# Tree attention: SyncE's store of heads 76 to 79 is cut by partitions for two heads instead of four

## The chip, the cores and the metric

The kernel runs on one core of a Trainium2 chip. A core has TensorE (PE) for matrix products, VectorE (DVE), ScalarE (ACT), GpSimd (POOL) and SyncE (SP), which only issues transfers and waits, and 16 DMA engines that move data between the chip's main memory and the core's on-chip memory. That on-chip memory has 128 partitions. SyncE, ScalarE and GpSimd each have a queue of transfers; all queues run on the same 16 DMA engines. In the profile q0 is GpSimd's queue (software_dynamic), q1 SyncE's and q10 ScalarE's (hardware_dynamic).

The metric is the device time of one execution in microseconds (us); lower is better. The kernel before takes 135.0 us, the median of three runs between 134.7 and 135.12 us.

## The reference

There are 8 x 12 = 96 heads, each with 512 positions of dimension 64. The mask is a binary tree: position i attends to itself and to its ancestors.

```python
for i in range(seq):
    mask[i, i] = 1
    parent = i
    while parent > 0:
        parent = (parent - 1) // 2
        mask[i, parent] = 1
scores = einsum('bhqd,bhkd->bhqk', Q, K) * scale + (1 - mask) * (-1e9)
weights = softmax(scores)
return einsum('bhqk,bhkd->bhqd', weights, V).astype(float32)
```

Inputs and output are float32, 96 x 512 x 64 each, 12.58 MB.

## The kernel before, in words

A position is written 4p + t: partition p holds positions 4p to 4p + 3 of a head. So one head's output takes 128 rows of 4 x 64 floats, one row of 1024 bytes for each partition, and a row is contiguous in main memory.

The heads are worked in 48 pairs. The main loop runs over i from 0 to 48. A step S computes the scores of pair i on TensorE (mask codes enter as a matrix product, `scores1` and `scores2`) and their exponentials on ScalarE; a step V multiplies the weights of pair i - 1 with its values (`values`, L661) and normalises (`norm`: reciprocal L691, multiplication L693, both on VectorE), which leaves float32 results in a tile `of`; steps K and Q turn keys and queries for later pairs. From pair 16 on, pair i holds heads 8(i // 4) + i % 4 and the one four above it, so that four pairs make eight consecutive heads, and these share one `of` tile.

The order is written out by hand; the program's text is the order on each engine. GpSimd loads all but the first inputs by a list of operations (`pool_program`), and issues the stores of finished groups of eight heads on its queue. Each operation on that list is issued once `ready` allows it.

The stores of the end are divided. GpSimd stores heads 72 to 75 (512 KB) and, last, heads 80 to 87 (1024 KB). SyncE stores the rest of the group in between, heads 76 to 79 (`APART` = 76), after step i = 41 (`APART_AT`), by `store_apart` (L711 to L714): one transfer for partitions 0 to 59 (`APART_ROWS` = 60) of all four heads, and one for the 68 partitions from 60 on. At steps 45, 46 and 47 SyncE stores two heads each (88 and 92, 89 and 93, 90 and 94), and after the loop head 91, while ScalarE stores head 95. SyncE's queue holds nothing else in this stretch; its transfers run in the order in which they are issued. At the end of the program SyncE waits for the stores (L918). All stores are issued by the helper `store`, so all have line L701.

The `of` tiles come from a pool of 11 buffers for 12 groups of heads, so the last group takes the buffer that the first group's store has left.

Of the kernel before, what the change touches and what calls it, by code (L numbers as in the profile page):

```python
# [119 lines left out]
def kernel(  # L120
# [7 lines left out]
    nc = tc.nc  # L128
# [571 lines left out]
    def store(eng, h0, n, step=1, p0=0, p1=P):  # L700
        return eng.dma_start(  # L701
            out=Or[p0:p1, h0:h0 + step * (n - 1) + 1:step, :],
            in_=ofs[h0 // 8][p0:p1, h0 % 8:h0 % 8 + step * (n - 1) + 1:step, :, :].rearrange(
                "p h t d -> p h (t d)"
            ),
        )


    APART, APART_AT, APART_ROWS = 76, 41, 60

    def store_apart():  # L711

        for p0, p1 in ((0, APART_ROWS), (APART_ROWS, P)):
            store(nc.sync, APART, 4, 1, p0, p1)  # L714

    def pool_program():

# [138 lines left out]
    for i in range(NP + 1):  # L856
# [29 lines left out]
        if i == APART_AT:  # L886
            store_apart()
# [35 lines left out]
```

## Time and profile before

| What | Value |
|---|---|
| Median of three runs | 135.0 us (134.7 to 135.12) |
| The profiled execution's own time | 134.66 us |
| Its span, first to last instruction | 132.9 us |
| TensorE busy | 114.7 us, 86% of the span |
| VectorE, ScalarE, GpSimd busy | 104.8, 101.1, 82.9 us |
| Read from and written to main memory | 37.94 MB and 12.58 MB, 380 GB/s over the span |
| SyncE's two transfers for heads 76 to 79 | issued from 111.66 us on, 240 KB and 272 KB |

Times inside the profile count from the span's start. A row of the timeline gives start, duration, engine, line and operation; a q behind an engine's name means its sequencer, which issues transfers. A row of DMA issues gives what goes where, the issuing engine, how many, the size of each, and the median time from issue to landing; it gives no landing where the records do not tell one. A row of a queue gives its packets, the megabytes, and the packets' time as a share of all 16 DMA engines' time in that stretch. A row of windows gives the stretch, the busy time of each engine with its instruction count, the clock granted to TensorE, and after it the mean busy share of the 16 DMA engines and what they moved in GB/s. Packet times in the records overlap by a few ns, so a share can stand slightly above the truth.

### The profile page before, as it was taken

What the parts mean: (1) busy time and instruction counts of PE and PEld (TensorE: products, weight loads), DVE (VectorE), ACT (ScalarE), POOL (GpSimd) and SP (SyncE); (2) the same over time, 40 slices, a digit from 0 to 9 for tenths busy, and PEclk for the clock granted to TensorE, in tenths of its full rate; (3) what the DMA queues carried; (4) which work ended last, traced back from release to release, by engine and by line L of the source; (5) the groups of instructions that cost most, each with busy time, mean ns of one, the idle gap of its engine ahead of it and who ended that gap; (6) DMA issues with size and microseconds to landing.
All of it is one profiled execution on the core that took longest, in us unless ns stands there. A gap on an engine that the chain in (4) does not pass through costs nothing.

```text
span 132.9 us, 5421 instructions
## 1 busy us (share of the span) xinstructions
PE 114.7 (86%) x2350; PEld 79.9 (60%) x2353; DVE 104.8 (79%) x254; ACT 101.1 (76%) x163; POOL 82.9 (62%) x114
## 2 busy tenths in 40 slices
PE   6983999999899798899999898994999999999900
PEld 2441677667576476667676675773676677775600
DVE  3436769988999998989899889896999977974530
ACT  4356469989799986969997797985799778789800
POOL 6968734345493999994399999926998935002000
PEclk9999599999999999999999999999999999999995
DMA  3999999999999999999999999999999999999980
GB/s 96 238 177 195 195 199 199 202 201 207 202 202 211 204 210 203 208 208 202 209 206 200 328 249 203 310 263 263 311 231 341 219 334 404 399 400 361 381 306 32
DMA packets 28092, 32.25 MB, mean 243 GB/s; under 512 B 1149, under 2 KB 23293, under 8 KB 28069
## 3 DMA queue, kind: packets, MB, share of 16 engines
q0 software_dynamic: 25696, 29.63, 109.9%
q1 hardware_dynamic: 1813, 1.83, 4.0%
q10 hardware_dynamic: 560, 0.46, 1.2%
q8 instruction: 18, 0.29, 0.8%
q14 instruction: 5, 0.04, 0.1%
HBM read 37.94 MB, written 12.58 MB: 380 GB/s over the span
## 4 chain that ended last, share of the span: by engine, by line
DMA 28%; PE 27%; DVE 19%; POOL 13%; issue 5%; ACT 4%; ACTq 0%; POOLq 0%
DMA qst<-in_Q_dram 19%; PE ob L661 9%; DMA vst<-in_V_dram 8%; POOL vt L370 7%; DVE of L693 6%; DVE vt L370 5%; PE s L566 4%; PE s L573 2%; DVE rec L691 2%; DVE kq L485 2%; PE ktp L469 2%; POOL kst L243 2%; PE s L611 2%; PE s L600 2%; DVE kq L489 1%
## 5 line engine op out<-in xcount | busy, mean ns | idle before, releaser
L583 ACT ACTIVATE e<-s 128x1024 bf16<-128x1024 f32 x40 | 40.9, 1023 | 14.0 <-PE s L573 13.6
L661 PE MATMUL ob<-vt,e 128*128 128x65 bf16 (+1 forms) x940 | 37.5, 198 | 2.7 <-DVE of L693 2.0
L661 PEld LDWEIGHTS <-e 128*128 128x128 bf16 (+1 forms) x960 | 30.5, 103 | 11.4 <-PE s L611 1.9
L370 POOL COPY vt<-vst 32x512 int32<-32x512 int32 (+4 forms) x44 | 32.4, 736 | 4.1 <-PE ob L661 1.9
L617 ACT ACTIVATE e<-s 128x384 bf16<-128x384 f32 x80 | 34.7, 491 | 0.0
L693 DVE TENSOR_TENSOR of<-ob,rec 128x512 f32<-128x512 f32 x47 | 32.5, 691 | 1.6
L370 DVE COPY vt<-vst 32x1024 bf16<-32x1024 bf16 (+5 forms) x47 | 22.8, 486 | 2.7 <-DMA vst<-in_V_dram 1.8
L691 DVE RECIPROCAL rec<-ob 128x8 f32<-128x8 f32 x47 | 9.6, 203 | 10.8 <-PE ob L661 9.7
L701 POOL DMA_DIRECT2D out_dram<-of x11 | 9.8, 892 | 9.2 <-DVE of L693 8.8
L573 PE MATMUL s<-qq,kq 64*128 64x512 bf16 x80 | 15.3, 377 | 0.0
L611 PEld LDWEIGHTS <-kq 64*128 64x128 bf16 x320 | 12.3, 94 | 4.1
L611 PE MATMUL s<-qq,kq 64*128 64x160 bf16 (+1 forms) x320 | 14.7, 208 | 0.0
L253 POOL DMA_DIRECT2D qst<-in_Q_dram x12 | 8.5, 705 | 6.8 <-DMA kst<-in_K_dram 3.2
L566 PE MATMUL s<-far,codes 40*128 40x512 bf16 x64 | 12.5, 386 | 0.1
L600 PEld LDWEIGHTS <-codes 40*128 40x128 bf16 x80 | 6.3, 95 | 9.7 <-issue 3.8
L542 DVE COPY qq<-qtp 128x1024 bf16<-128x1024 bf16 x16 | 10.9, 681 | 1.6 <-PE qtp L537 1.6
L370 ACT COPY vt<-vst 32x512 int32<-32x512 int32 (+3 forms) x19 | 10.4, 546 | 2.1 <-DMA vst<-in_V_dram 1.7
L579 ACT ACTIVATE e<-s 128x1024 bf16<-128x1024 f32 x8 | 8.2, 1022 | 5.0 <-PE s L573 4.8
L600 PE MATMUL s<-far,codes 40*128 40x384 bf16 x64 | 10.6, 324 | 0.5 <-ACT e L617 0.3
L476 PE MATMUL ktp<-ptile,kst 128*64 128x128 bf16 x256 | 10.1, 220 | 0.9 <-DMA kst<-in_K_dram 0.5
L253 POOL DMA_DIRECT2D kst<-in_K_dram x11 | 8.4, 768 | 3.9 <-DMA vst<-in_V_dram 1.9
L537 PE MATMUL qtp<-ptile,qst 128*64 128x128 bf16 x192 | 7.6, 220 | 2.5 <-DMA qst<-in_Q_dram 1.8
(56 smaller groups left out, 154.4 us busy)
## 6 DMA issues: line engine op xcount, KB each, us to landing
out_dram<-of POOLq DMA_DIRECT2D x10, 1024.0 KB, 15.7
kst<-in_K_dram POOLq DMA_DIRECT2D x9, 512.0 KB, 14.5
qst<-in_Q_dram POOLq DMA_DIRECT2D x8, 512.0 KB, 16.6
vst<-in_V_dram POOLq DMA_DIRECT2D x12, 256.0 KB, 12.9
vst<-in_V_dram POOLq DMA_DIRECT2D x6, 512.0 KB, 12.5
qst<-in_Q_dram POOLq DMA_DIRECT2D x6, 256.0 KB, 12.0
kst<-in_K_dram POOLq DMA_DIRECT2D x4, 256.0 KB, 9.7
out_dram<-of SPq DMA_DIRECT2D x3, 256.0 KB, 6.0
```

The lines of the kernel that those rows point to most:

```text
L253: return nc.gpsimd.dma_start(out=kept[b][:, h0 % KB:h0 % KB + n, :, :].rearrange("p (g x) t d -> p g (x t d)", x=x), in_=src[:, h0 // x:(h ...
L370: return copy(out=dst, in_=src)
L542: nc.vector.tensor_copy(out=qqs[j][:, :, 8 * last:8 * last + 8, :].rearrange("p b u c -> p b (u c)"), in_=quarters,)
L566: nc.tensor.matmul(out=sp[:, a, :], lhsT=(k1code if i < WIDE else k1wide)[64 * a:64 * a + CODE_ROWS, :], rhs=(q1code, q1wide, q1far)[(i >= ...
L573: nc.tensor.matmul(out=sp[:, a, :], lhsT=keys(i, a, TOP), rhs=qTs[i][64 * a:64 * a + 64, :, :].rearrange("p t c -> p (t c)"), start=False, ...
L583: ) if i < WIDE else nc.scalar.activation(
L600: nc.tensor.matmul(out=flat[:, a, :, :].rearrange("p u (t c) -> p u t c", t=4)[:, :, :, 32 // n:], lhsT=k2wide[64 * a:64 * a + CODE_ROWS, ...
L611: nc.tensor.matmul(out=flat[:, a, :, lo:hi], lhsT=keys(i, a, WTILE2[t]), rhs=qT[64 * a:64 * a + 64, :, lo:hi], start=False, stop=t == 1, s ...
L617: nc.scalar.activation(out=e2s[i % NE][:, a, :, 32:128].rearrange("p t (r u) -> p t r u", u=n), in_=flat[:, a, :, :].rearrange("p u (t r) ...
L661: nc.tensor.matmul(out=ob[lo:hi, a, 65 * t:65 * t + 65], lhsT=e[:, a, PLACE[t], lo:hi], rhs=vt[vtile[tile_v][0]][:, head(i, a) % VB, vtile ...
L691: nc.vector.reciprocal(out=rec[:, a:a + n, :, :], in_=o4[:, a:a + n, :, D:D + 1])
L693: nc.vector.tensor_tensor(out=ofs[j][:, h0:h1 + 1:head(i, 1) - head(i, 0), :, :], in0=o4[:, a:a + n, :, 0:D], in1=rec[:, a:a + n, :, :].to ...
```

## The change

SyncE's two transfers by partitions (0 to 59 and 60 to 127) now carry two heads each, 76 and 77, instead of four. A third transfer is added behind them on the same queue: heads 78 and 79, all 128 partitions in one. What is stored, where to, the place in the program and the issuing engine stay.

```diff
     def store_apart():
 
         for p0, p1 in ((0, APART_ROWS), (APART_ROWS, P)):
-            store(nc.sync, APART, 4, 1, p0, p1)
+            store(nc.sync, APART, 2, 1, p0, p1)
+        store(nc.sync, APART + 2, 2)
```

On SyncE's list of instructions the two transfers of 60 and 68 partitions times four heads become transfers of 60 and 68 partitions times two heads, and one of 128 partitions times two heads follows. The instructions of the other engines and their order are the same in both kernels.

## The prediction

> **What bounds the kernel now.** The change lies in the last 21 us, so I read the page's counts and slices only for the end, then the chain that ended last, then the DMA queues, and last the end in short windows.
>
> ```profile
> span 132.9 us, 5421 instructions
> PE 114.7 (86%) x2350; PEld 79.9 (60%) x2353; DVE 104.8 (79%) x254; ACT 101.1 (76%) x163; POOL 82.9 (62%) x114
> DMA  3999999999999999999999999999999999999980
> ```
>
> TensorE leads by busy share, and the DMA engines are full until the last two of the 40 slices. The busy shares do not say what ends last. The chain's last pieces, the page's issue rows and SyncE's waits do:
>
> ```profile
> 125.20 1.10 PE s L661 x20
> 126.33 0.19 DVE rec L691
> 126.55 0.42 DVE of L693
> 126.97 0.10 DVE rec L691
> 127.09 0.42 DVE of L693
> ...
> 127.55 0.35 ACTq L701 DMA_DIRECT2D out_dram<-of  x1
> ...
> out_dram<-of SPq DMA_DIRECT2D x1, 128.0 KB, 4.5
> out_dram<-of ACTq DMA_DIRECT2D x1, 128.0 KB, 4.1
> ...
> SPq L918 <- DMA out_dram<-of: 3.7, 4, 1.5
> ```
>
> The last arithmetic ends at 127.09 + 0.42 = 127.51. ScalarE issues the last store at 127.55 and it lands 4.1 us later, at about 131.65. SyncE then has only its waits for stores (L918, 3.7 us in four). From 127.5 to 132.9 no compute runs: 5.4 us of the span are stores draining. The chain names VectorE last, because a store has no successor on an engine; the end itself is a matter of DMA. A 128 KB store alone would not need 4.1 us, so I look at how many of the 16 DMA engines still work (share times 16):
>
> ```profile
> core 0: us, PE busy (x) PEld busy (x) DVE busy (x) ACT busy (x) POOL busy (x), PEclk, DMA share, GB/s
> 129.00:129.25 0.25, 0.00 (x0) 0.00 (x0) 0.00 (x0) 0.00 (x0) 0.00 (x0) 1.00 0.59 201
> 129.25:129.50 0.25, 0.00 (x0) 0.00 (x0) 0.00 (x0) 0.00 (x0) 0.00 (x0) 0.83 0.43 148
> 129.75:130.00 0.25, 0.00 (x0) 0.00 (x0) 0.00 (x0) 0.00 (x0) 0.00 (x0) 0.50 0.25 86
> 130.25:130.50 0.25, 0.00 (x0) 0.00 (x0) 0.00 (x0) 0.00 (x0) 0.00 (x0) 0.50 0.14 49
> 130.50:130.75 0.25, 0.00 (x0) 0.00 (x0) 0.00 (x0) 0.00 (x0) 0.00 (x0) 0.50 0.14 49
> 131.00:131.25 0.25, 0.00 (x0) 0.00 (x0) 0.00 (x0) 0.00 (x0) 0.00 (x0) 0.50 0.11 37
> 131.25:131.50 0.25, 0.00 (x0) 0.00 (x0) 0.00 (x0) 0.00 (x0) 0.00 (x0) 0.50 0.01 4
> ```
>
> Shares of 0.59, 0.43, 0.25 and 0.14 are 9.4, 6.9, 4.0 and 2.2 engines. Most have moved their last byte by about 129.3, a second group of two or so works until about 130.0, and two engines alone go on to 131.25, at 49 / 2 = 24.5 GB/s each. A packet here is one head's row of one partition, 1024 bytes, so it costs 1024 / 24.5 = 41.8 ns. **The bound is the backlog of the two fullest DMA engines**, some 1.25 us behind the second group.
>
> **Why engines are unequally full.** The stores of this stretch, and SyncE's queue (q1) beside POOL's (q0) in the 2 us from 116 and from 119.6:
>
> ```profile
> out_dram<-of SPq DMA_DIRECT2D x1, 272.0 KB
> out_dram<-of SPq DMA_DIRECT2D x1, 240.0 KB, 9.0
> ...
> 111.66 1.10 SPq L701 DMA_DIRECT2D out_dram<-of  x2
> ...
> q0 software_dynamic: 166, 0.63, 80.1%
> q1 hardware_dynamic: 158, 0.16, 22.8%
> ...
> q0 software_dynamic: 179, 0.68, 86.2%
> q1 hardware_dynamic: 48, 0.05, 6.8%
> ```
>
> Both parts are issued from 111.66 on, the 60-partition part (240 KB) first; it lands 9.0 us later, at 120.7. From 116 to 118 the queue moves 158 packets, 79 per us, which is the 60-partition part. From 119.6 to 121.6, with the 68-partition part (272 packets) left, it moves 48, only 24 per us, although POOL's queue is as busy as before and nothing else has changed. So the second part lies on far fewer engines. Each engine gives the two queues turns. With the first part on 15 engines (60 rows, four each) one engine moves 79 / 15 = 5.3 packets per us, and 24 / 5.3 gives 4.6 engines. I take that stores are dealt in whole rows and evenly; then 68 rows can go on four engines (17 rows each), and not on five or six. So each of four engines has 17 x 4 = 68 packets of this part, where each of the 15 has 16 of the other.
>
> The Trainium skill, "DMA: Bandwidth & Descriptors", section "Why a DMA increments its semaphore by 16 and not by 1", states that a store from SyncE goes on the largest number of engines up to 16 that divides the size of the slowest dimension, the lowest-numbered ones. By that rule 60 gives 15 and 68 gives 4, the 128-partition store gives 16, and the four are among the fifteen. The trace's 24 packets per us against 79 agree in size; no row names an engine.
>
> **The change part by part.**
>
> *Bytes and issues.* The same 512 KB leave. SyncE issues three stores where it issued two:
>
> ```profile
> L701 SPq DMA_DIRECT2D out_dram<-of x6: 356/502/826, 111.7 to 127.0; - x6
> ...
> 122.47 0.40 SPq L701 DMA_DIRECT2D out_dram<-of  x1
> ...
> firstK<-in_K_dram SPq DMA_DIRECT2D x1, 256.0 KB, 3.2
> ```
>
> One issue more costs 0.36 to 0.83 us of SyncE's time. The two end at 112.76, so the third ends by 113.6 at the latest, and SyncE's next one starts only at 122.47, after a wait for VectorE. The 8.9 us between cover it; without this cover it would be paid once, before the first of the last stores. No wait for data is added: the first issue's wait for VectorE covers all four heads already. With one transfer more the semaphores of SyncE's queue are taken again one store earlier, so the stores of the loop's last three steps, of which one has waited for a transfer of the kernel's start to be done, will have two that do; that transfer landed 3.2 us after its issue at the span's start, so the wait costs nothing. Nothing on POOL, ScalarE, VectorE or TensorE moves.
>
> *60 partitions of two heads instead of four.* Each of 15 engines has 8 packets instead of 16: 8 x 41.8 ns = 0.33 us less.
>
> *68 partitions of two heads instead of four.* Each of the four has 34 instead of 68: 34 x 41.8 = 1.42 us less.
>
> *128 partitions of two heads, new.* 256 packets over 16 engines: 16 x 41.8 = 0.67 us more on every engine.
>
> Sum per engine: the four go from 84 packets to 58, so -26 x 41.8 = **-1.09 us**; eleven go from 16 to 24, +0.33 us; the sixteenth goes from none to 16, +0.67 us. If the 68 rows lay on the 4.6 engines of the raw rate, the four would have 59 before and 30 after, -21 packets, -0.88 us; that is the other bound for this term, and 1.09 is taken since only four engines share 68 rows evenly.
>
> *Does an engine's end move by the whole of its packets?* It does where the engine never idles between the third store and the end. The slices say so: DMA is at 9 tenths to slice 38. A queue that POOL fills late can leave an engine idle for a moment, but the four have the backlog of the 68-partition part and so are the last to run dry. Nor does another wait begin: a store's buffer is not reused here (11 buffers for 12 groups of eight heads, only the last group takes an old one, from the first store), and the inputs were loaded before.
>
> *What is late next.* If the two engines that end at 131.25 are of the four, they end at 131.25 - 1.09 = 130.16. The second group, which ends at about 130.0, either is of the four as well (then 128.9) or of the eleven (then 130.0 + 0.33 = 130.33). Most engines end at 129.3 + 0.33 = 129.6. So the last byte moves from 131.25 to between 130.16 and 130.33. I take 130.33, since the second group stands nearer to the many: **0.92 us earlier**. Landing (0.4 us after the last byte) and the program's end stay as they are.
>
> *The sum.* The profiled execution took 134.66 us with a span of 132.9; it becomes 133.7. It stands 0.34 below the median of the runs, 135.0, and below all three. Moved by the same 0.92, the median becomes 134.1, which is my forecast. By the bounds of the terms alone (0.88 to 1.09) it would be 133.9 to 134.1.
>
> **What speaks for the step that carries it.** That the last two engines are of the four is inferred, not read. Every other store of this stretch has 128 partitions, so it gives each engine the same bytes; the 68-partition part alone gives four engines 68 - 16 = 52 packets, 2.2 us, above the even deal of the other part's 16, and two engines are 131.25 - 129.3 = 1.95 us behind most. POOL's queue points the same way. From 127.45 to 128.7 it still moves 12 packets of 4 KB:
>
> ```profile
> q1 hardware_dynamic: 357, 0.34, 77.3%
> q0 software_dynamic: 12, 0.05, 9.7%
> ```
>
> 12 packets in 1.25 us are too few for more than two or three engines. So a couple of engines were late with POOL's last store as well, as they would be if the 68 packets had taken turns with it. Against it speaks that four engines carry those packets and only two are that late.
>
> **The rivals.**
>
> *Slower: the two late engines are not of the four.* Their lag would then be in POOL's own queue, which moves 12 late packets on them. They have 16 packets of the changed store now and would have 24 (+0.33 us), or none and then 16 (+0.67): 134.66 goes to 135.0 or 135.3 by the profile, and the median of 135.0 to 135.3 or 135.7. It decides as soon as one engine outside the four ends after 131.25 - 0.33 = 130.9. For it: two late, not four. Against it: the size of the lag fits the 68 packets. The Trainium skill, the same page, section "Latency and other measured facts", says that DMA engines 7 and 15 are usually slower than the others, for stores that GpSimd issues; were the two late ones those, this rival would hold. No row here names them.
>
> *Less gain: the sixteenth engine ends last.* If the second group holds the engine that has no packet of the 60-partition part, it goes from 130.0 to 130.67 and the gain is 0.58: 134.4. For it: nothing but its place in the count, one in twelve per engine. Against it: with fewest packets it should run ahead.
>
> *No change: the lag varies.* If the two engines fell behind by chance, and in other executions the ends lie level at about 130, the -1.09 on the four is worth what remains above the eleven's +0.33, near nothing: 134.8 to 135.2. The three runs lie 0.4 us apart, so the end does not vary by more than that, which speaks against it.
>
> **How the numbers follow.** Forecast 0.53 (134.1, its own range 133.5 to 134.5), less gain 0.12 (134.4), no change 0.15 (135.0), slower 0.20 (135.3 to 135.7). A measurement of this kernel tells about 0.3%, 0.4 us, from no change. The forecast and the lesser gain lie beyond that, so faster is 0.65, the same 0.15, slower 0.20. The range goes from 133.5 (the profiled time with the full 1.09) to 135.3, where the first half of the slower rival is in.
>
> **What would show it.** Right: the last stretch with a share of 0.14 (two engines) is gone or under 0.4 us, the share falls from 0.9 to nothing in about 1.2 us instead of 2.3, and ScalarE's last store lands in about 3.2 us instead of 4.1. SyncE issues three stores before 113.6. q1's second rate (24 per us) ends some 3 us sooner. Wrong: two engines still run on to 131.25 or beyond, or a tail of one engine remains; then the late engines were others than the four. If the compute ends at another time than 127.51, something moved that I say does not.

## The result, and the profile after

In the comparison that the forecast is held against, the changed kernel takes 133.55 us (median) against 134.85 us before: a ratio of 0.9903 with a 95% interval from 0.9875 to 0.9932, so 0.9 to 1.7 us faster. Three later comparisons of the same two kernels, on three different chips and each with 11 or 12 runs of the change against 23 to 33 of before, give 0.998, 0.9979 and 0.9983: faster by about 0.2%, 0.23 to 0.28 us. The interval of the first of these three (0.9953 to 1.0006) touches 1. Ratios and intervals leave out the few executions in which the chip was in a slower state. Both are results; the second is the better measured.

The profiled execution of the changed kernel took 133.59 us, with a span of 131.7 us. Its chain ends with VectorE, and then ScalarE issues the last store. The timeline of SyncE's stores, in two stretches, shows when they are issued (start, duration, engine, line, operation, count):

```profile
126.03 0.10 DVE rec L691
126.16 0.42 DVE of L693
...
126.61 0.35 ACTq L701 DMA_DIRECT2D out_dram<-of  x1
```

```profile
106.37 0.78 SPq L701 DMA_DIRECT2D out_dram<-of  x2
...
110.72 15.69 SPq L701 DMA_DIRECT2D out_dram<-of  x5
```

The transfers of heads 76 and 77 are issued at 106.37, that of heads 78 and 79 at 110.72. Before, both transfers were issued from 111.66 on. The prediction had them all stay at that moment.

The two issues, and the end in short windows (last column but one: mean busy share of the 16 DMA engines):

```profile
out_dram<-of SPq DMA_DIRECT2D x1, 136.0 KB
...
out_dram<-of SPq DMA_DIRECT2D x1, 120.0 KB, 7.4
```

```profile
128.00:128.50 0.50, 0.00 (x0) 0.00 (x0) 0.00 (x0) 0.00 (x0) 0.00 (x0) 0.50 0.87 305
129.00:129.25 0.25, 0.00 (x0) 0.00 (x0) 0.00 (x0) 0.00 (x0) 0.00 (x0) 0.50 0.32 111
129.75:130.00 0.25, 0.00 (x0) 0.00 (x0) 0.00 (x0) 0.00 (x0) 0.00 (x0) 0.50 0.13 45
130.00:130.25 0.25, 0.00 (x0) 0.00 (x0) 0.00 (x0) 0.00 (x0) 0.00 (x0) 0.50 0.09 29
130.25:130.50 0.25, 0.00 (x0) 0.00 (x0) 0.00 (x0) 0.00 (x0) 0.00 (x0) 0.50 0.00 0
```

The last byte leaves at about 130.2 instead of 131.25. That looks like the forecast. But the last arithmetic ends at 126.16 + 0.42 = 126.58, 0.93 us earlier than before (127.51), and from there to the last byte it is 3.6 us, against 3.7 before. The profiles gained that 0.93 us earlier in the program. TensorE's wait for a load of queries, from the timeline of before and of the changed kernel:

```profile
92.32 0.64 PE L537 MATMUL qtp<-ptile,qst 128*64 128x128 bf16 x16 [1.58 <-DMA qst<-in_Q_dram]
```

```profile
91.41 0.64 PE L537 MATMUL qtp<-ptile,qst 128*64 128x128 bf16 x16 [0.85 <-DMA qst<-in_Q_dram]
```

This turn of queries starts 0.91 us earlier, 15 us ahead of anything that the change touches. So this one pair of profiles cannot carry the forecast's explanation, however well its end fits.

### The profile page after: what moved, and what is told of

The parts are those of the page before. It is cut to its first block, busy times and chain, and to the rows that moved or that the text cites. A ratio compares the mean times of both kernels' runs of the same rounds, so it can differ in the third digit from the quotient of the medians.

```text
span 131.7 us, 5422 instructions
## 1 busy us (share of the span) xinstructions
PE 113.8 (86%) x2350; PEld 79.8 (61%) x2353; DVE 103.6 (79%) x254; ACT 101.0 (77%) x163; POOL 83.1 (63%) x114
## 4 chain that ended last, share of the span: by engine, by line
DMA 30%; PE 30%; DVE 15%; POOL 9%; ACT 7%; issue 4%; ACTq 0%; POOLq 0%
DMA qst<-in_Q_dram 14%; DMA kst<-in_K_dram 11%; PE ob L661 10%; POOL vt L370 6%; DMA vst<-in_V_dram 5%; DVE of L693 5%; PE s L566 4%; DVE vt L370 3%; PE s L573 3%; ACT e L617 3%; PE s L600 2%; PE s L611 2%; ACT vt L370 2%; PE qtp L531 2%; PE ktp L469 2%
## 5 line engine op out<-in xcount | busy, mean ns | idle before, releaser
L370 DVE COPY vt<-vst 32x1024 bf16<-32x1024 bf16 (+5 forms) x47 | 21.4, 456 | 3.1 <-DMA vst<-in_V_dram 2.2
L298 POOL DMA_DIRECT2D vst<-in_V_dram x7 | 5.6, 800 | 5.8 <-DMA vst<-in_V_dram 4.0
```

Of the source, the lines that this page charges most:

```text
L370: return copy(out=dst, in_=src)
```

## The experiments

All edits are in `store_apart`. "Late" means that nothing is issued before head 79 is normalised, "early" that heads 76 and 77 go when they are ready.

**1. Both kernels once more.** No edit.

> The kernel before, unchanged, for a second profile of it. Backlog theory (the time is set by the two DMA engines left with the 68-partition part): the time is that of the kernel before within 0.3%, the last arithmetic to the last landing takes about 4.1 us, and two engines alone work on for 1 us or more at the end. Rival, the moment of the loads: the last arithmetic comes at a time that differs from one execution to the next by up to 1 us, whatever the stores do, and the profile shows it 0.5 us or more away from 127.5 us.

> The changed kernel, unchanged, for a second profile of it. Backlog theory: 0.9 to 1.3 us faster than before, whichever moment the last arithmetic comes at. Rival, the moment of the loads: the last arithmetic comes anywhere between 126.5 and 127.6 us, and the gain with it lies anywhere between 0.2 and 1.3 us.

The kernel before against itself: 0.9982 (0.9953 to 1.0012), 134.04 us. The changed kernel: 0.998 (0.9953 to 1.0006), 134.05 us. The gain of the first comparison did not come back, and the unchanged kernel lies as far below 1 here as the changed one, so this comparison alone does not tell the two apart. The last arithmetic of these two profiles ended at 126.96 and 127.71, so it moves from one execution to the next, as the rival had it. The rows of c_before and of c_after, and two rows of c_before's end:

```profile
126.54 0.42 DVE of L693
```

```profile
127.29 0.42 DVE of L693
```

```profile
130.25:130.50 0.25, 0.00 (x0) 0.00 (x0) 0.00 (x0) 0.00 (x0) 0.00 (x0) 0.50 0.13 45
130.75:131.00 0.25, 0.00 (x0) 0.00 (x0) 0.00 (x0) 0.00 (x0) 0.00 (x0) 0.50 0.07 25
```

The backlog theory expected two engines alone for 1 us or more at the end of c_before. There is a stretch of two engines (0.13 x 16 = 2.1), and then of one (0.07 x 16 = 1.1). So the tail of the kernel before differs by execution too.

**2. The dose: packets on the four engines.** One transfer for all (32 packets on every engine), and three heads by partitions (71 on four).

```diff
-        for p0, p1 in ((0, APART_ROWS), (APART_ROWS, P)):
-            store(nc.sync, APART, 4, 1, p0, p1)
+        store(nc.sync, APART, 4)                          # h0
```

```diff
-            store(nc.sync, APART, 4, 1, p0, p1)
+            store(nc.sync, APART, 3, 1, p0, p1)           # h3
+        store(nc.sync, APART + 3, 1)
```

> Heads 76 to 79 in one transfer of 128 partitions, so 32 packets on each DMA engine: against the kernel before, 52 packets fewer on the four engines, 16 more on eleven, 32 more on one. Backlog theory: the four no longer end last; the eleven do, 16 x 41.8 ns = 0.67 us later than before, so at 130.0 + 0.67 = 130.7 instead of 131.25: 0.5 to 0.6 us faster than before, 0.3 to 0.4 slower than the changed kernel. Rival, the moment of the loads: no order among these kernels; this one lies within 0.4 us of the changed kernel on either side. Rival, the count of transfers: one transfer fewer than before, so at least as fast as the changed kernel.

> The transfers by 60 and 68 partitions carry three heads, the one of 128 partitions one: 71 packets on the four engines, where before has 84 and the changed kernel 58. Backlog theory: 13 x 41.8 ns = 0.54 us faster than before and as much slower than the changed kernel. Rival, the moment of the loads: no difference from the changed kernel beyond 0.3 us that is in this order. Rival, the count of transfers: three as in the changed kernel, so as fast as it.

h0: 1.0022 (0.9994 to 1.005), 134.52 us. h3: 0.9967 (0.9941 to 0.9992), 134.0 us. The backlog theory wanted h0 0.5 us faster than before; it is if anything slower. And the end of h0's profile has what the theory ascribed to the 68-partition part:

```profile
129.00:129.50 0.50, 0.00 (x0) 0.00 (x0) 0.00 (x0) 0.00 (x0) 0.00 (x0) 0.50 0.41 141
130.00:130.50 0.50, 0.00 (x0) 0.00 (x0) 0.00 (x0) 0.00 (x0) 0.00 (x0) 0.50 0.13 47
130.50:130.75 0.25, 0.00 (x0) 0.00 (x0) 0.00 (x0) 0.00 (x0) 0.00 (x0) 0.50 0.14 49
131.00:131.25 0.25, 0.00 (x0) 0.00 (x0) 0.00 (x0) 0.00 (x0) 0.00 (x0) 0.50 0.01 4
```

From 130.0 to 131.0 two engines (0.13 x 16 = 2.1) work alone, although every store of this stretch has 128 partitions here, the same bytes for every engine. So two late engines do not prove an uneven store. The forecast had read them as members of the four.

The other two expectations for h0 missed as well: it is 0.47 us behind the changed kernel (134.52 against 134.05), more than the 0.4 us that the moment of the loads allowed, and its one transfer does not make it as fast.

h3 has more packets on the four than the changed kernel and is no slower (134.0 against 134.05), where the backlog theory expected it 0.54 us behind. It also issues its first two transfers earlier than before does (from 108.47 on in its profile), so it does not separate packets from moment.

**3. The issue's moment apart from the packets.** The changed kernel's packets, all late; an even spread with the changed kernel's moments; and the changed kernel again.

```diff
+        store(nc.sync, APART + 2, 2)                      # late, late2
         for p0, p1 in ((0, APART_ROWS), (APART_ROWS, P)):
-            store(nc.sync, APART, 4, 1, p0, p1)
+            store(nc.sync, APART, 2, 1, p0, p1)
```

```diff
-        for p0, p1 in ((0, APART_ROWS), (APART_ROWS, P)):
-            store(nc.sync, APART, 4, 1, p0, p1)
+        for p0, p1 in ((0, 64), (64, P)):                 # even3
+            store(nc.sync, APART, 2, 1, p0, p1)
+        store(nc.sync, APART + 2, 2)
```

> The changed kernel, unchanged, once more. So far it measured 0.9903 of the kernel before in one comparison and 0.998 in another. Balance theory (the four engines with the 68-partition part and the other twelve end within about 0.5 us of each other in both kernels, and which of them is last differs by execution): 0.1 to 0.4 us faster than before. Rival, the first comparison is the rule: 0.9 to 1.3 us faster.

> The three transfers of the changed kernel in another order: 128 partitions of heads 78 and 79 first, then 60 and 68 partitions of heads 76 and 77. The packets of each engine are those of the changed kernel, but nothing is issued before head 79 is normalised, about 4.4 us later than the changed kernel issues its first two. Balance theory: as the changed kernel within 0.3 us. Rival, the earlier issue is what gains: slower than the changed kernel by 0.3 us or more, at the time of the kernel before.

> Three transfers at the changed kernel's moments, but by 64 and 64 partitions, so that every engine has 32 packets as with one transfer of 128 partitions. Balance theory: as that kernel, 0.3 us slower than before and 0.5 us slower than the changed kernel. Rival, the earlier issue is what gains: as fast as the changed kernel.

The changed kernel: 0.9979 (0.9964 to 0.9995), 133.87 us. late: 1.0002 (0.9979 to 1.0025), 134.1 us. even3: 1.0002 (0.9978 to 1.0027), 134.28 us, with h0's packets but early. Both expectations for even3 missed: it is not as fast as the changed kernel, and not 0.3 us slower than before. The packets of the change without its early issue bring nothing that can be measured; but the intervals of late and the changed kernel overlap, hence the repeat below.

even3's profiled execution (134.25 us) shows something else. The last arithmetic's row of h3 (133.69 us) and of even3, even3's last store, and its end:

```profile
126.08 0.42 DVE of L693
```

```profile
129.13 0.42 DVE of L693
...
129.58 0.35 ACTq L701 DMA_DIRECT2D out_dram<-of  x1
```

```profile
130.50:130.75 0.25, 0.00 (x0) 0.00 (x0) 0.00 (x0) 0.00 (x0) 0.00 (x0) 0.50 1.03 369
130.75:131.00 0.25, 0.00 (x0) 0.00 (x0) 0.00 (x0) 0.00 (x0) 0.00 (x0) 0.50 0.36 115
131.00:131.25 0.25, 0.00 (x0) 0.00 (x0) 0.00 (x0) 0.00 (x0) 0.00 (x0) 0.50 0.00 0
```

In even3 the arithmetic ended at 129.55, 3 us later than in h3 (126.50) and 2 us later than in the profile of before, and all 16 engines stop together at about 130.85; yet its time is within 0.6 us of h3's, and the kernel before's median in the same comparison is 134.15. Here the end does hang on the arithmetic: the last store is issued at 129.58, and the last byte leaves 1.3 us after the last arithmetic, where before and after have 3.7 and 3.6 us from the last arithmetic to the last byte. The late arithmetic of this execution cost about what its short and level tail gave back. The third profile of the changed kernel (c_after3, below) ends in the same way, with the arithmetic at 129.33 and 134.1 us. So the moment of the last arithmetic alone does not tell the time: in all profiles of this document but two34's it lies between 126.5 and 129.6, and their times between 133.6 and 134.7 us, not in the same order.

**4. The price of packets on an engine.** The 68-partition part cut in two of 34.

```diff
-        for p0, p1 in ((0, APART_ROWS), (APART_ROWS, P)):
+        for p0, p1 in ((0, APART_ROWS), (APART_ROWS, 94), (94, P)):   # two34
             store(nc.sync, APART, 4, 1, p0, p1)
```

> The kernel before with its 68-partition part cut in two of 34 partitions, so that by whole rows two engines carry 136 packets of it where four had 68; the other two lose theirs. If the four engines set the end of the kernel before: two of them get 68 x 41.8 ns = 2.84 us more, and the time grows by all of it, 2.8 us. Balance theory: they are up to 0.5 us short of the end, 2.3 to 2.8 us slower. Rival, the late engines are others than the four and end 1.5 us or more behind them: 1.3 us slower or less.

1.0148 (1.0121 to 1.0175), 136.29 us; 0.0148 x 134.15 = 1.99 us slower. Its end:

```profile
130.00:130.50 0.50, 0.00 (x0) 0.00 (x0) 0.00 (x0) 0.00 (x0) 0.00 (x0) 0.50 0.27 94
131.00:131.50 0.50, 0.00 (x0) 0.00 (x0) 0.00 (x0) 0.00 (x0) 0.00 (x0) 0.50 0.13 47
131.50:132.00 0.50, 0.00 (x0) 0.00 (x0) 0.00 (x0) 0.00 (x0) 0.00 (x0) 0.50 0.13 47
132.00:132.25 0.25, 0.00 (x0) 0.00 (x0) 0.00 (x0) 0.00 (x0) 0.00 (x0) 0.50 0.06 21
```

Two engines run to 132.0 and one beyond. So a part of few partitions does lie on few engines, and packets piled on them do set the end once there are enough. By the rule of the Trainium skill, "DMA: Bandwidth & Descriptors", section "Why a DMA increments its semaphore by 16 and not by 1", 34 partitions lie on two engines; the 0.13 fits that. But 68 packets more cost 1.99 us and not the 2.84 that 68 x 41.8 ns make. If a packet costs these two engines that much, they end 0.85 us short of the end in the kernel before. It is an estimate for the average execution, and it lies between the theories: expected were 2.3 to 2.8 us if they nearly set the end, 1.3 or less if they were far from it.

**5. The two causes crossed.** The kernel before's packets, early; late again; the changed kernel a third time; and 71 packets on the four, early.

```diff
-        for p0, p1 in ((0, APART_ROWS), (APART_ROWS, P)):
-            store(nc.sync, APART, 4, 1, p0, p1)
+        for h in (0, 2):                                  # early84
+            for p0, p1 in ((0, APART_ROWS), (APART_ROWS, P)):
+                store(nc.sync, APART + h, 2, 1, p0, p1)
```

```diff
-        for p0, p1 in ((0, APART_ROWS), (APART_ROWS, P)):
-            store(nc.sync, APART, 4, 1, p0, p1)
+        for h, n in ((0, 2), (2, 1)):                     # early71
+            for p0, p1 in ((0, APART_ROWS), (APART_ROWS, P)):
+                store(nc.sync, APART + h, n, 1, p0, p1)
+        store(nc.sync, APART + 3, 1)
```

> The changed kernel a third time. Two comparisons with 11 and 12 undisturbed runs gave 0.998 and 0.9979, the first with 5 gave 0.9903. If the small one is the rule: between 0.996 and 1.000. If the chip decides: as the first, below 0.993, on a chip where the kernel before runs near 134.9 us.

> The changed kernel's packets, all issued after head 79 (a repeat of the run late, 1.0002). If the spread over the engines gains: as the changed kernel within 0.15%. If the earlier issue of two heads gains: as the kernel before within 0.15%, 0.2% above the changed kernel.

> The kernel before's packets (84 on four engines, 16 on eleven, none on one), but by two heads at a time: 60 and 68 partitions of heads 76 and 77 as early as in the changed kernel, then 60 and 68 of heads 78 and 79. If the earlier issue gains: as the changed kernel, 0.998. If the spread gains: as the kernel before, 1.000, or slower by the issue of one transfer more. If both gain by halves: 0.999.

> As the changed kernel, but head 78 too goes by 60 and 68 partitions, so 71 packets on the four engines, with heads 76 and 77 issued early. It joins what the two fastest kernels so far have. If the balance of engines and the earlier issue both gain: 0.996 to 0.998. If more transfers cost: above the changed kernel.

The changed kernel: 0.9983 (0.9971 to 0.9995), 134.02 us. late2: 0.9991 (0.9972 to 1.0011), 133.95 us. early84: 0.997 (0.9958 to 0.9982), 133.79 us. early71: 0.9963 (0.9951 to 0.9975), 133.65 us, the fastest of all: clearly ahead of the kernel before, and ahead of the change by 0.2%, where the two intervals just overlap. It lies where a gain from both causes was expected, but early84 is as fast within the intervals. late2 does not decide: it lies within 0.15% of the kernel before and of the changed kernel, and its median is even 0.07 us below the changed kernel's. The crossed table of ratios:

| Packets on four / eleven / one engine | late | early |
|---|---|---|
| 84 / 16 / 0 | 1 (the kernel before; against itself 0.9982) | 0.997 (early84) |
| 58 / 24 / 16 | 1.0002, 0.9991 (late, late2) | 0.998, 0.9979, 0.9983 (the change) |
| 32 / 32 / 32 | 1.0022 (h0) | 1.0002 (even3) |

Along every row the early issue gains 0.1 to 0.3%. Down a column, 58 instead of 84 packets on the four gains nothing (0 to 0.1% late, 0.1% the wrong way early), and 32 loses about 0.2%. The single steps are as large as the intervals, so each by itself is weak. The firmest is that early84, with the kernel before's own packets, lies clear of 1. It has four transfers instead of two, but the number of transfers alone does not gain: late, late2 and even3 have three, as the change has, and are no faster than before. That the early issue gains is therefore the better supported reading, not a settled one. SyncE's issues of late2 and early84, with the end of each:

```profile
111.23 1.88 SPq L701 DMA_DIRECT2D out_dram<-of  x3
```

```profile
130.00:130.50 0.50, 0.00 (x0) 0.00 (x0) 0.00 (x0) 0.00 (x0) 0.00 (x0) 0.50 0.08 27
130.50:131.00 0.50, 0.00 (x0) 0.00 (x0) 0.00 (x0) 0.00 (x0) 0.00 (x0) 0.50 0.06 23
131.00:131.25 0.25, 0.00 (x0) 0.00 (x0) 0.00 (x0) 0.00 (x0) 0.00 (x0) 0.50 0.03 8
```

```profile
106.35 5.69 SPq L701 DMA_DIRECT2D out_dram<-of  x4
```

```profile
130.00:130.25 0.25, 0.00 (x0) 0.00 (x0) 0.00 (x0) 0.00 (x0) 0.00 (x0) 0.50 0.12 41
130.25:130.50 0.25, 0.00 (x0) 0.00 (x0) 0.00 (x0) 0.00 (x0) 0.00 (x0) 0.50 0.05 16
130.50:131.00 0.50, 0.00 (x0) 0.00 (x0) 0.00 (x0) 0.00 (x0) 0.00 (x0) 0.50 0.00 0
```

With 58 packets on the four and a late issue, one engine works alone until about 131.1; with 84 and an early issue the last one is done by about 130.5. One execution each, but it is the opposite order of what the packets alone would give.

**Which engines end last.** No view names a DMA engine, but the trace records for each store of SyncE when each engine that has a share of it reports this share as landed. The kernel before has 15 such reports for its 60-partition part and four for its 68-partition part, and two34 has two for each part of 34. So the deal of packets that the prediction took is what the trace shows.

The four can be followed one store further. An engine that takes packets of SyncE and of POOL in turns needs, for the next store's 16 packets and 16 of POOL's, about 16 x (41.8 + 159 ns) = 3.2 us; the 159 ns are the mean time of POOL's packets in the last section's row of q0 (1.014 x 16 x 3.6 us / 368). In four profiles each report of the four has one of the next store 3.2 to 3.3 us behind it (times in us):

| Profile | The four report the 68-partition part | The next store, 3.2 to 3.3 us later | Its last two reports of 16 | Last landing of all |
|---|---|---|---|---|
| before | 124.10, 125.01, 126.27, 126.43 | 127.33, 128.25, 129.52, 129.67 | 129.52, 129.67 | 131.67 |
| c_before | 124.11, 124.65, 124.86, 126.24 | 127.34, 127.90, 128.11, 129.49 | 128.97, 129.49 | 131.50 |
| late | 123.06, 123.57, 123.76, 123.93 | 126.32, 126.81, 127.01, 127.19 | 128.97, 129.42 | 131.40 |
| late2 | 122.84, 123.58, 123.77, 125.11 | 126.09, 126.83, 127.04, 128.36 | 128.46, 129.45 | 131.43 |

By this matching, which is an inference, both late engines of the profile before were of the four, as the prediction had read them; in c_before only the last one was. In late and late2, with the changed kernel's packets, the four are through earlier, and two other engines end last, about as late as the four had. On this reading that is why the shift of packets gains so little. Which engines these others are, and why they are late, is not shown.

## Why the prediction was right or wrong, point by point

*The time and the sign.* 134.1 us was forecast, 133.55 measured in the comparison at the start, 133.87 to 134.05 in the later ones; faster in each, though one of the intervals touches 1. The size, 0.92 us, lies at the lower edge of the first difference (0.9 to 1.7 us) and is over three times the later ones (0.23 to 0.28 us). Right in time and sign, but by luck: the reason is one that the runs do not bear out.

*"the first issue's wait for VectorE covers all four heads already."* This step failed. The first issue's wait covers what that transfer reads. With two heads instead of four it was met at 106.37, 4.4 us before that of heads 78 and 79. The prediction took the wait to belong to the place in the program and not to what each transfer reads. The crossed table points here for the gain.

*"the four go from 84 packets to 58, so -26 x 41.8 = -1.09 us."* The packets are real: 120 and 136 KB went instead of 240 and 272, and the reports confirm 15 and four engines. That the kernel's end follows the four's end by nearly all of it is the other step that failed. late and late2 make the same shift of packets without the early issue and gain 0 and 0.1% (0.12 us). Their four engines end earlier, and two others end last, at 131.40 and 131.43 where before and c_before have 131.67 and 131.50. two34 puts the two engines that it loads 0.85 us short of the end on average.

*"That the last two engines are of the four is inferred, not read."* For the execution that the prediction read, the reports bear the inference out. Its argument does not hold in general: in h0 two engines are late by about a microsecond with equal bytes, and in c_before one of the late two is none of the four. The rival in which the late engines are not of the four was given 0.20. The time that it gave (slower by 0.33 us or more) did not come; but late and late2 end as it describes, and early84 is faster than the change, as it would be if the packets that move to the other engines cost something there. No comparison here is fine enough to show that. The rival "no change: the lag varies", given 0.15, is nearest to the later comparisons. Against it the prediction set that three runs lay 0.4 us apart; in the comparison with h0 the undisturbed runs of the kernel before lie between 133.55 and 135.47 us. The gain of 0.58 of the rival with the sixteenth engine was measured nowhere. The Trainium skill, "DMA: Bandwidth & Descriptors", section "Latency and other measured facts", has DMA engines 7 and 15 as usually slower than the others, which would give two late engines; no run here names them.

*"What would show it."* It came in part. The last byte came about 1.05 us earlier, and the stretch of two engines shrank to under 0.5 us. But the share still took about 2 us from 0.87 to nothing (from 128.25 to 130.25) where 1.2 us was forecast, and ScalarE's last store, issued at 126.61, had its last byte only at about 130.2, where its landing was forecast for 3.2 us after the issue. And the sign that something else had moved was there: compute ended at 126.58, not at 127.51. The earlier last byte was misleading, since the profiled execution of the changed kernel was ahead by 0.91 us at 91.4 already. A sign that also follows from an earlier start should have been stated relative to the last arithmetic; there it was 3.6 us against 3.7.

*The third issue's cost.* Nothing, as forecast: SyncE's three issues end at 111.1, and early71 with five of them is the fastest.

*What stays open.* Why the early issue gains some 0.1 to 0.4 us, where the DMA engines are full before and after it, is not settled: no run separates "earlier" from "behind other work in the queues". Nor is it known why two engines outside the four are late, or why the first comparison gave 1.0%, on a chip that is not known; there before was 0.6 to 0.7 us slower and the change 0.3 to 0.5 us faster than in all later ones.

## What to carry to other kernels

When a transfer is cut into smaller ones, ask for each piece what it waits for: the piece may go earlier, and that can be worth more than the new shape. A tail in which few DMA engines still work tells that engines are unequally full, not which store made them so; an equal spread as a control (here h0) tells at once whether the tail needs an uneven store, and the engines' own reports of each store tell more than the tail does. And where the time of one execution to the next varies by as much as the effect, a single pair of profiles can show the expected picture by chance: compare a stretch from a mark inside it, and repeat the comparison before explaining its size.

## What the runs showed of the hardware that was not expected

The first transfer of SyncE was issued at 111.66 in the kernel before, and from 111.7 to 115.3 its queue moved no packet at all, while POOL's queue held the engines:

```profile
DMA packets 368, 1.43 MB, mean 397 GB/s; under 512 B 19, under 2 KB 19, under 8 KB 368
## 3 DMA queue, kind: packets, MB, share of 16 engines
q0 software_dynamic: 368, 1.43, 101.4%
```

So here a store that was issued into full engines waited some 3.6 us before its first byte, and took turns only then. The early issue of the changed kernel did not escape this: issued at 106.37, its first transfer has no packet in the stretch from 106 to 109 either. And instruction loading shares the engines. From 117.5 to 119.5 of the profile of before:

```profile
q1 hardware_dynamic: 123, 0.11, 16.4%
q8 instruction: 1, 0.02, 3.1%
```

One packet of queue q8 takes 0.031 x 16 x 2 us = 1.0 us of one engine. That is about the lag of the late engines in h0, and a candidate for it; no run here tested it.
